# One decoder layer on one core: order of the products of the first two quads, and of norm, transposes and splits in the output projection

## The chip, the cores and the metric

The kernel runs on one core of a Trainium2 chip, in one program. The metric is the time of one execution on the device in microseconds (us); the time of a kernel is the median of its runs. A core has five engines with a queue of instructions each: TensorE (PE in the profile, with its weight loads as PEld), VectorE (DVE), ScalarE (ACT), GpSimd (POOL) and SyncE (SP, which here only issues transfers). An engine works its queue off in order, and an instruction waits until the instructions of other engines that it depends on have ended.

## The reference

One layer of a decoder with 512 tokens and a model width of 1024, in float32. Only the last third matters here:

```python
mixed = (sigmoid(gate_a) * (o_nsa @ w_branch_a) + sigmoid(gate_b) * (z @ w_branch_b))
x = x + mixed @ w_out                       # output projection, 512x1024 @ 1024x1024
h = rms_norm(x, norm2_g)
return x + square(relu(h @ w_up)) @ w_down  # D_FF = 4096
```

## The kernel before

Each float32 operand is kept as a high part and a low part, and each product of two operands is three matmuls (`mm3`, lines 230 to 232): high by high, high by low, low by high. A weight is loaded by SyncE into `w_raw`; ScalarE copies it into `w_hi` (line 87) and VectorE subtracts to get `w_lo` (line 89). This pair is called a split below. The weights of the last two stages are split in one piece of 128x1024.

The order of all work is the order in which the Python code emits it (a manual schedule): each engine gets its instructions in the order of the text, and the places are fixed by hand. `later(k, f)` emits `f` k slots on; in the quads a slot is one step of three matmuls, and a product of a quad is 8 slots.

**Output projection** (`tok_gemm`, `o_second`, `h_chunk`). The second half of its columns is computed token chunk by token chunk (c = 0 to 3, 128 tokens each, 24 matmuls of 512 columns). When chunk c is done, `after` is `o_second`: VectorE adds the residual (`x`, line 857), ScalarE squares and sums (line 905), small operations make the scale `st` (lines 907, 193 to 195) and VectorE writes the normed chunk `hn` (line 909). `mid(c - 1)` is `h_chunk` of the chunk before: TensorE transposes `hn` into `ptr` (line 919, 8 transposes, two PSUM tiles), ScalarE copies them to `ht` and `hA` (lines 922, 927) and VectorE subtracts for the low part of `hA` (line 928). For c = 1 and 2 `mid(c - 1)` is emitted at the end of product c and ahead of `after(c)`; for c = 3 it is emitted after three quarters of the product. Four splits of weights of the next stage are emitted at (c, kp) = (2, 1), (2, 3), (3, 0) and (3, 1).

**Up stage** (`up_group`, class `Quad`). The up and down matmuls use a seven-product scheme (Strassen-Winograd): a quad makes four blocks of h @ w_up from seven products p1 to p7 of 24 matmuls of 256 columns each. Three accumulators in PSUM carry them: `y` takes p1, p6, p7 and p4 one on top of the other, `z` takes p5 and p3, `x` takes p2. Between two products on the same accumulator its value is read out: `keep` copies it (p1, p5 and u2; line 1002, ScalarE), and `block` subtracts (line 1026, VectorE) and then queues square, high part and low part of the result (lines 1011 to 1020). So a product that goes on in `y` or `z` waits until ScalarE's copy or VectorE's block has read it. Group 0 (g = 0) has two quads a and b that are interleaved, because their input `h` is not ready at the start: the sums S1 to S4 of parts of `h` (`h_sum`, line 934, in `ht`) and their high and low parts (`h_parts`, lines 938 and 939, in `hS`) are made while p1 and p2 of both quads run. Then the products follow as a.p5, a.p6, a.p3, a.p7, b.p5, a.p4, b.p6, b.p3, b.p7, b.p4. The blocks of a quad lie in one tile `G` with a single buffer, so b's first write to `G` waits for a's last read of it; the block of p2 lies in `a11` (two buffers). After p4 four sums over blocks (S1, S2, S4, S3; line 1070, VectorE) make the inputs of the down stage, `uh` and `ul`.

**Down stage** (`st_down`): the same scheme with matmuls of 512 columns, accumulators `dacc`. Groups 1 to 3 follow in the same way, one quad after the other.

Of the kernel before, what the change touches and what calls it, by code (L numbers as in the profile page):

```python
# [104 lines left out]
def layer(tc, flat, sizes, x, cst, wck, wcv, g1, g2, out):  # L105
# [36 lines left out]
    for g in range(4):  # L142
        for what in ("u", "d"):
            b11, b12, b21, b22 = (W.dram(2048) for _ in range(4))
            t1, t2, t3, t4 = t = [
                dr.tile([P, 2048], F32, name=f"t{what}{k + 1}_{g}") for k in range(4)
            ]
            sums.append([[m[:, v : v + 1024] for m in (b11, b12, b22, b21, *t)]
                         for v in (0, 1024)])

            def half(c, *ms):
                return [m[:, c * 1024 : (c + 1) * 1024] for m in ms]

            if what == "d":
                for m in (b11, b21, t1, t2, b22, t3, t4):
                    W.plan += half(0, m) + half(1, m)
            elif g:
                for c in range(2):
                    W.plan += half(c, b11, t1, t2, b22, t3, b21, t4)
            else:  # L160
                W.plan += half(0, b11, b21) + half(1, b11, b21) + half(0, t1, t2, b22, t3)
                W.plan += half(1, t1) + half(0, t4) + half(1, t2, b22, t3, t4)


    xs = [sp.tile([P, DM], F32, name=f"x{c}") for c in range(NT)]
# [62 lines left out]
    def mm3(ps, a, b, start, stop, **kw):  # L228

        nc.tensor.matmul(ps, a[0], b[0], start=start, stop=False, **kw)  # L230
        nc.tensor.matmul(ps, a[0], b[1], start=False, stop=False, **kw)  # L231
        nc.tensor.matmul(ps, a[1], b[0], start=False, stop=stop, **kw)  # L232
# [624 lines left out]
        nc.vector.tensor_tensor(v, ps, v, ALU.add)  # L857
        return v

    def tok_gemm(ci, act, after, tok_outer, last=False, mid=None):  # L860

        if not tok_outer:
            acc = [ps_acc.tile([P, 512], F32, name="acc", tag="acc") for _ in range(NT)]
            for kp in range(4):
                hi, lo = W.get(ci + kp)
                W.split_to(ci + kp + 2)
                for k in range(2):
                    ko = 2 * kp + k
                    w = slice(k * 512, (k + 1) * 512)
                    tick(2.9)  # L870
                    for c in range(NT):
                        mm3(acc[c], part(act, ko, c), (hi[:, w], lo[:, w]),
                            ko == 0, ko == NKO - 1)
                        if ko == NKO - 1:
                            after(c, acc[c])
        else:
            for c in range(NT):
                parts = 2 if last and c == NT - 1 else 1
                for b in range(parts):
                    n = 512 // parts  # L880
                    ps = ps_acc.tile([P, 512], F32, name="acc", tag="acc")
                    for kp in range(4):
                        hi, lo = W.get(ci + kp)
                        for k in range(2):
                            ko = 2 * kp + k
                            w = slice(k * 512 + b * n, k * 512 + (b + 1) * n)
                            mm3(ps[:, :n], part(act, ko, c), (hi[:, w], lo[:, w]),
                                ko == 0, ko == NKO - 1)
                        tick(1.45 / parts)
                        if (c, kp) in ((2, 1), (2, 3), (3, 0), (3, 1)):  # L890
                            W.split_to(W.ns)
                        if kp == (2 if c == NT - 1 else 3) and b == parts - 1 and c:
                            mid(c - 1)
                    if parts == 1:
                        after(c, ps)
                    else:
                        after(c, ps[:, :n], b * n, n)

    def o_first(c, ps):
        v = res_add(c, 0, ps)  # L900
# [74 lines left out]
    class Quad:  # L975
# [48 lines left out]
        def block(self, v, d, a, b, op, k=0):  # L1024

            nc.vector.tensor_tensor(d, a, b, op)  # L1026
            later(2, lambda: self.square(d))
            later(4 + k, lambda: self.high(v, d))
            later(6 + k, lambda: self.low(v, d))

# [22 lines left out]

        def p7(self):
            self.mm(self.y, S3, False)
            self.block(A22, self.g(A22), self.t["p5"], self.y, ALU.subtract)

        def p4(self):
            self.mm(self.y, A22, False)
            a21 = self.g(S3)  # L1060
            nc.scalar.activation(a21, self.y, AF.Relu)
            if self.q < 2:
                nc.scalar.activation(a21, a21, AF.Square)
            else:
                nc.vector.scalar_tensor_tensor(
                    a21, self.y, 0.0, a21, op0=ALU.max, op1=ALU.mult
                )

            def sum_(d, a, b, op):
                nc.vector.tensor_tensor(self.g(d), a, b, op)  # L1070

            def parts(k, a, b=None):
                v = slice(a, (b or a) + 1)
                src = self.G[:, :, v.start - 1 : v.stop - 1, :]
                later(k, lambda: self.high(v, src))
                later(k + 2, lambda: self.low(v, src))

            later(1, lambda: sum_(S1, a21, self.g(A22), ALU.subtract))
            later(3, lambda: sum_(S2, self.g(S1), self.a11, ALU.subtract))
            parts(4, S1)  # L1080
            later(5, lambda: sum_(S4, self.g(S2), self.g(A12), ALU.add))
            later(7, lambda: sum_(S3, self.a11, a21, ALU.subtract))
            parts(9, S2, S4)
            parts(11, S3)
# [4 lines left out]
    def up_group(g):  # L1089
        each[0] = 0.36  # L1090
        a, b = Quad(2 * g), None
        if g:
            for q in range(2):
                a = a or Quad(2 * g + q)
                for f in (a.p1, a.p5, a.p6, a.p3, a.p7, a.p2, a.p4):
                    f()
                a = None
            return

        t2, t3 = slice(0, P), slice(P, 2 * P)  # L1100
        later(3, lambda: h_parts(S1, t2))
        later(5, lambda: h_sum(S3, 0, 2, ALU.subtract, t2))
        a.p1()
        a.p2(24)
        b = Quad(1)
        h_chunk(NT - 1)
        h_sum(S1, 2, 3, ALU.subtract, t3)
        h_parts(S1, t3)
        later(3, lambda: h_sum(S3, 0, 2, ALU.subtract, t3))
        later(5, lambda: h_sum(S2, 3, 0, ALU.subtract))  # L1110
        later(7, lambda: h_parts(S2))
        later(10, lambda: h_sum(S4, 0, 1, ALU.add))
        later(12, lambda: h_parts(S4))
        later(15, lambda: h_parts(S3))
        later(16, open_act)
        b.p1()
        b.p2(24)
        for f in (a.p5, a.p6, a.p3, a.p7, b.p5, a.p4, b.p6, b.p3, b.p7, b.p4):
            f()

    def st_down(ci, last):
# [181 lines left out]
```

## Time and profile before

| | before |
|---|---|
| time, median of 3 runs | 821.95 us (820.93 to 822.28) |
| the profiled execution, its own time | 820.94 us |
| span of the profiled execution, first to last instruction | 819.2 us |
| busy time of TensorE / VectorE / ScalarE | 790.5 / 585.3 / 396.2 us |

The span lies 1.7 us inside the execution's own time, and this execution is 1.0 us under the median. Times in rows are microseconds from the start of the span. A matmul's duration in a row holds its pipeline; the distance of two starts is what a matmul costs: a row of 256 columns lasts 0.28 us, and the next one starts 0.12 us after it.

### The profile page before, as it was taken

To read this page: it belongs to the slowest core of one execution; us is meant where nothing else is said; L and a number is where in the kernel's file an instruction comes from. 1 tells how busy PE (TensorE), PEld (TensorE's weight loads), DVE (VectorE), ACT (ScalarE), POOL (GpSimd) and SP (SyncE) were. 2 spreads that over 40 slices of the span, in tenths; PEclk is the share of its full clock that TensorE was granted. 3 is DMA by queue.
4 is the path that set the end of the run, shared out by engine and by line. 5 is a ranking of instruction groups with operands and counts; after the bars stand their busy time and mean duration, and the time that the engine had idled before them with its cause. 6 is when DMAs were issued, how large, how long until landed. Compare 5 with 4: busy or idle time off the path is not lost.

```text
span 819.2 us, 11917 instructions
## 1 busy us (share of the span) xinstructions
PE 790.5 (97%) x4421; PEld 681.2 (83%) x4421; DVE 585.3 (71%) x1005; ACT 396.2 (48%) x714; POOL 88.2 (11%) x138
## 2 busy tenths in 40 slices
PE   5999989999999999999999987979999999999998
PEld 4898868888888788888888777968998899889987
DVE  6577887666767466665666478778599769967984
ACT  5544645545455353223223456863465446535651
POOL 0011573224323200000000000000000000000000
PEclk9999999999999999999999999989999999999999
DMA  9346568568757749999999822537988995565562
GB/s 343 122 133 202 139 130 207 173 159 171 193 154 133 175 120 323 317 323 324 349 324 319 324 83 98 180 129 217 290 254 260 255 268 192 186 199 189 181 208 78
DMA packets 49450, 172.56 MB, mean 211 GB/s; under 512 B 5616, under 2 KB 6000, under 8 KB 49392
## 3 DMA queue, kind: packets, MB, share of 16 engines
q1 hardware_dynamic: 42768, 148.14, 52.8%
q0 software_dynamic: 4608, 16.78, 13.3%
q10 hardware_dynamic: 2016, 6.88, 2.4%
q8 instruction: 35, 0.57, 0.3%
q14 instruction: 23, 0.19, 0.1%
HBM read 152.90 MB, written 52.43 MB: 251 GB/s over the span
## 4 chain that ended last, share of the span: by engine, by line
PE 86%; DVE 7%; ACT 4%; issue 1%; DMA 1%; POOL 0%; SPq 0%; ACTq 0%; DVEq 0%; POOLq 0%
PE acc L230 14%; PE acc L232 14%; PE acc L231 14%; PE dacc L230 6%; PE dacc L232 6%; PE dacc L231 6%; PE uacc L230 4%; PE uacc L231 4%; PE uacc L232 4%; PE ptu L687 2%; PE sc L640 2%; PE uz L230 2%; PE uz L231 2%; PE uz L232 2%; PE pv L711 1%
## 5 line engine op out<-in xcount | busy, mean ns | idle before, releaser
L89 DVE TENSOR_TENSOR w_lo<-w_raw,w_hi 128x512 fp32r<-128x512 f32 (+3 forms) x268 | 233.9, 887 | 76.9 <-ACT w_hi L87 76.1
L87 ACT ACTIVATE w_hi<-w_raw 128x512 fp32r<-128x512 f32 (+3 forms) x268 | 201.3, 778 | 99.7 <-PE dacc L232 71.1
L230 PE MATMUL acc<-xh,w_hi 128*128 128x512 f32 x336 | 137.5, 409 | 0.0
L232 PE MATMUL acc<-xh,w_lo 128*128 128x512 f32 x336 | 131.7, 392 | 0.0
L231 PE MATMUL acc<-xl,w_hi 128*128 128x512 f32 x336 | 131.1, 390 | 0.0
L231 PE MATMUL dacc<-w_lo,uh 128*128 128x512 f32 (+1 forms) x228 | 87.9, 386 | 0.0
L230 PE MATMUL dacc<-w_hi,uh 128*128 128x512 f32 (+1 forms) x228 | 87.9, 386 | 0.0
L232 PE MATMUL dacc<-w_hi,ul 128*128 128x512 f32 (+1 forms) x228 | 87.8, 385 | 0.0
L232 PEld LDWEIGHTS acc<-xh,w_lo 128*128 128x128 f32 x336 | 63.0, 188 | 14.3
L230 PEld LDWEIGHTS acc<-xh,w_hi 128*128 128x128 f32 x336 | 63.2, 188 | 11.8 <-issue 3.2
L231 PEld LDWEIGHTS acc<-xl,w_hi 128*128 128x128 f32 x336 | 63.3, 188 | 8.0
L230 PE MATMUL uacc<-hA,w_hi 128*128 128x256 f32 x192 | 55.4, 289 | 4.7 <-DVE G L1026 4.7
L652 ACT ACTIVATE p<-p,nst 128x512 f32<-128x512 f32 (+2 forms) x48 | 29.6, 616 | 55.7 <-DVE nst L648 54.5
L231 PE MATMUL uacc<-hA,w_hi 128*128 128x256 f32 x192 | 55.2, 288 | 0.0
L232 PE MATMUL uacc<-hA,w_lo 128*128 128x256 f32 x192 | 55.2, 288 | 0.0
L232 PEld LDWEIGHTS dacc<-w_hi,ul 128*128 128x128 f32 x228 | 42.8, 188 | 8.7
L231 PEld LDWEIGHTS dacc<-w_lo,uh 128*128 128x128 f32 x228 | 42.8, 188 | 8.5
L230 PEld LDWEIGHTS dacc<-w_hi,uh 128*128 128x128 f32 x228 | 42.8, 188 | 8.4
L1132 DVE TENSOR_TENSOR x<-x,dacc 128x512 f32<-128x512 f32 (+1 forms) x57 | 36.8, 673 | 11.5 <-PE dacc L232 11.5
L693 DVE TENSOR_TENSOR pt<-ptu,pt 128x384 fp32r<-128x384 f32 (+1 forms) x48 | 28.8, 600 | 19.6 <-ACT pt L692 19.5
L668 POOL TENSOR_SCALAR p<-p,nst 128x512 f32<-128x512 f32 (+2 forms) x48 | 32.8, 690 | 88.6 <-DVE nst L666 43.5
L230 PEld LDWEIGHTS uacc<-hA,w_hi 128*128 128x128 f32 x192 | 37.8, 197 | 5.0 <-DVE G L1026 4.9
(231 smaller groups left out, 1659.4 us busy)
## 6 DMA issues: line engine op xcount, KB each, us to landing
w_raw<-w_flat SPq DMA_DIRECT2D x110, 512.0 KB, 4.7
w_raw<-tu SPq DMA_DIRECT2D x32, 512.0 KB, 4.8
w_raw<-td SPq DMA_DIRECT2D x32, 512.0 KB, 4.7
tu<-w_flat SPq DMA_DIRECT2D x16, 512.0 KB, 6.3
z<-w_flat SPq DMA_DIRECT2D x16, 512.0 KB, 6.8
tu<-w_flat POOLq DMA_DIRECT2D x8, 512.0 KB, 7.5
tu<-tu POOLq DMA_DIRECT2D x8, 512.0 KB, 9.6
td<-w_flat SPq DMA_DIRECT2D x8, 512.0 KB, 5.5
```

What stands on the lines that cost most here:

```text
L87: nc.scalar.activation(hi[:, v], t[:, v], AF.Copy)
L89: nc.vector.tensor_tensor(lo[:, v], t[:, v], hi[:, v].bitcast(F32), ALU.subtract)
L230: nc.tensor.matmul(ps, a[0], b[0], start=start, stop=False, **kw)
L231: nc.tensor.matmul(ps, a[0], b[1], start=False, stop=False, **kw)
L232: nc.tensor.matmul(ps, a[1], b[0], start=False, stop=stop, **kw)
L640: nc.tensor.matmul(ps[:, : b - a], QS[h][:, t], ks[h // 4][:, a:b], start=k == 0, stop=k == 1)
L652: later(1, lambda: nc.scalar.activation(p, p, AF.Exp, scale=-1.0, bias=mn, accum_out=sm))
L668: nc.gpsimd.tensor_scalar(p_of(u, k), p_of(u, k), nst[:, u % 4, 1, k : k + 1], 1.0, op0=ALU.mult, op1=ALU.mult,)
L687: nc.tensor.transpose(pt[:, n : n + P], p_of(u, c)[:, k * P : (k + 1) * P], ident)
L693: later(1, lambda: nc.vector.tensor_tensor(ptl[:, at], pt[:, :n], pth[:, at].bitcast(F32), ALU.subtract))
L711: nc.tensor.matmul(pv[:HD, q0:], v[:, :HD], ptl[:, at : at + w], start=False, stop=False)
L1132: nc.vector.tensor_tensor(v, v, ps[:, o : o + n], op)
```

## The change

1. In the output projection `mid(c - 1)` now comes behind `after(c)` for c = 1 and 2, and the splits are three instead of four, at (2, 0), (2, 1) and (3, 0). The unused handling of a half product is dropped.
2. The products of group 0 go a.p5, a.p6, a.p3, a.p7, b.p5, **b.p6, a.p4, b.p7, b.p3**, b.p4; the order in which the weights are loaded (`W.plan`) is changed to match.
3. `block` queues the square 2 + k // 2 slots on instead of 2. Only p2 of quads a and b has k = 24, so the squares of their first rows (`a11`) come 14 slots on.
4. The block of p7 goes into a tile `a22` of its own instead of a place in `G`, in all quads.

```diff
-                W.plan += half(1, t1) + half(0, t4) + half(1, t2, b22, t3, t4)
+                W.plan += half(1, t1, t2) + half(0, t4) + half(1, t3, b22, t4)
...
-                        if (c, kp) in ((2, 1), (2, 3), (3, 0), (3, 1)):
-                            W.split_to(W.ns)
-                        if kp == (2 if c == NT - 1 else 3) and b == parts - 1 and c:
-                            mid(c - 1)
-                    if parts == 1:
-                        after(c, ps)
-                    else:
-                        after(c, ps[:, :n], b * n, n)
+                    if (c, kp) in ((2, 0), (2, 1), (3, 0)):
+                        W.split_to(W.ns)
+                    if (c, kp) == (NT - 1, 2):
+                        mid(c - 1)
+                after(c, ps)
+                if 0 < c < NT - 1:
+                    mid(c - 1)
...
-            later(2, lambda: self.square(d))
+            later(2 + k // 2, lambda: self.square(d))
...
-            self.block(A22, self.g(A22), self.t["p5"], self.y, ALU.subtract)
+            self.a22 = gp2.tile([P, 2, 256], F32, name="a22", tag="a22")
+            self.block(A22, self.a22, self.t["p5"], self.y, ALU.subtract)
...
-            later(1, lambda: sum_(S1, a21, self.g(A22), ALU.subtract))
+            later(1, lambda: sum_(S1, a21, self.a22, ALU.subtract))
...
-        for f in (a.p5, a.p6, a.p3, a.p7, b.p5, a.p4, b.p6, b.p3, b.p7, b.p4):
+        for f in (a.p5, a.p6, a.p3, a.p7, b.p5, b.p6, a.p4, b.p7, b.p3, b.p4):
```

TensorE's own order in the output projection stays as it is, since `after` has no work for it. What moves there is VectorE's and ScalarE's order. VectorE's queue around the third chunk (`x_2`, `hn_4102`; `hn_4103` is the second chunk), before:

```order
L909 SCALAR_TENSOR_TENSOR hn_4103<-x_1_4094,st_4107,g2b 128x1024
L89 TENSOR_TENSOR w_lo<-w_raw,w_hi 128x1024 x2
L928 TENSOR_TENSOR hA_4092<-ptr,hA_4091 128x2x2x128 x2
L857 TENSOR_TENSOR x_2_4095<-acc,x_2_4095 128x512
L907 TENSOR_TENSOR st_4107<-st_4107 128x1
L193 TENSOR_SCALAR st_4107<-st_4107 128x1
L195 RECIPROCAL st_4107<-st_4107 128x1
L909 SCALAR_TENSOR_TENSOR hn_4102<-x_2_4095,st_4107,g2b 128x1024
L89 TENSOR_TENSOR w_lo<-w_raw,w_hi 128x1024 x2
```

and the same place of the changed kernel (its lines 857 and 89 are the same, 904 is the old 909, 923 the old 928):

```order
L904 SCALAR_TENSOR_TENSOR hn_4103<-x_1_4094,st_4107,g2b 128x1024
L923 TENSOR_TENSOR hA_4092<-ptr,hA_4091 128x2x2x128 x2
L89 TENSOR_TENSOR w_lo<-w_raw,w_hi 128x1024 x2
L857 TENSOR_TENSOR x_2_4095<-acc,x_2_4095 128x512
L902 TENSOR_TENSOR st_4107<-st_4107 128x1
L193 TENSOR_SCALAR st_4107<-st_4107 128x1
L195 RECIPROCAL st_4107<-st_4107 128x1
L904 SCALAR_TENSOR_TENSOR hn_4102<-x_2_4095,st_4107,g2b 128x1024
L923 TENSOR_TENSOR hA_4092<-ptr,hA_4091 128x2x2x128 x2
```

The `hA` pair ahead of `x_2` is that of the second chunk's transposes before, and of the first chunk's now; the second chunk's pair has moved behind `hn` of the third.

ScalarE's queue in the up stage, from the squares of a's first rows (`a_4557`) to the copy of a.p5's accumulator (`p_4694<-uz`), before; `a_4659` are b's first rows, and the three `hS` of 1024 elements are the high parts of S2, S4 and S3:

```order
L1011 ACTIVATE a_4557<-a_4557 128x512
L1012 ACTIVATE a_4557<-a_4557 128x512
L938 ACTIVATE hS_4491<-ht 128x1024
L1002 ACTIVATE p_4616<-uacc 128x512
L87 ACTIVATE w_hi<-w_raw 128x1024
L938 ACTIVATE hS_4491<-ht 128x1024 x2
L87 ACTIVATE w_hi<-w_raw 128x1024
L1011 ACTIVATE a_4659<-a_4659 128x512
L1012 ACTIVATE a_4659<-a_4659 128x512
L1002 ACTIVATE p_4694<-uz 128x512
```

and of the changed kernel, where `p_4692<-uz` is that copy and lines 1006 and 1007 are the squares:

```order
L933 ACTIVATE hS_4485<-ht 128x1024
L997 ACTIVATE p_4614<-uacc 128x512
L87 ACTIVATE w_hi<-w_raw 128x1024
L933 ACTIVATE hS_4485<-ht 128x1024
L1006 ACTIVATE a_4557<-a_4557 128x512
L1007 ACTIVATE a_4557<-a_4557 128x512
L933 ACTIVATE hS_4485<-ht 128x1024
L87 ACTIVATE w_hi<-w_raw 128x1024
L997 ACTIVATE p_4692<-uz 128x512
L87 ACTIVATE w_hi<-w_raw 128x1024
L1012 ACTIVATE uh<-a_4557 128x2x256
L1006 ACTIVATE a_4659<-a_4659 128x512
```

The squares of b's first rows have moved from ahead of the copy to behind it, and those of a's first rows from ahead of the high part of S2 to behind that of S4.

VectorE's queue between a's sums and b.p4, before; `G<-a_4557,G` is a's last sum, `G<-uz,u_4904` the block of b.p3 and `G<-p_4834,uacc` the block of b.p7, which b.p4 waits for:

```order
L1070 TENSOR_TENSOR G<-G 128x2x256
L1020 TENSOR_TENSOR ul<-G,uh 128x2x256
L1070 TENSOR_TENSOR G<-a_4557,G 128x2x256
L89 TENSOR_TENSOR w_lo<-w_raw,w_hi 128x1024
L1020 TENSOR_TENSOR ul<-G,uh 128x2x512
L1020 TENSOR_TENSOR ul<-G,uh 128x2x256
L1026 TENSOR_TENSOR G<-uz,u_4904 128x2x256
L89 TENSOR_TENSOR w_lo<-w_raw,w_hi 128x1024
L1020 TENSOR_TENSOR ul<-G,uh 128x2x256
L1026 TENSOR_TENSOR G<-p_4834,uacc 128x2x256
```

and of the changed kernel, where `a_4937<-p_4835,uacc` is the block of b.p7 and lines 1066 and 1015 are the old 1070 and 1020:

```order
L1066 TENSOR_TENSOR G<-G 128x2x256
L1015 TENSOR_TENSOR ul<-G,uh 128x2x256
L1066 TENSOR_TENSOR G<-a_4557,G 128x2x256
L1021 TENSOR_TENSOR a_4937<-p_4835,uacc 128x512
L89 TENSOR_TENSOR w_lo<-w_raw,w_hi 128x1024
L1015 TENSOR_TENSOR ul<-G,uh 128x2x512
L1015 TENSOR_TENSOR ul<-G,uh 128x2x256
L1015 TENSOR_TENSOR ul<-a_4937,uh 128x2x256
L1021 TENSOR_TENSOR G<-uz,u_4867 128x2x256
```

The block of b.p7 now stands directly behind a's last sum and ahead of the block of b.p3.

## Rows read from the trace of the kernel before

**Rows 1.** The page: the chain that ended last, shares by engine.
```profile
PE 86%; DVE 7%; ACT 4%; issue 1%; DMA 1%; POOL 0%; SPq 0%; ACTq 0%; DVEq 0%; POOLq 0%
```

**Rows 2.** Waits of PE, 430 to 580 us: total, times, longest.
```profile
PE uacc L230 <- DVE G L1026: 4.7, 1, 4.7
PE uz L230 <- ACT p L1002: 4.1, 1, 4.1
PE ptr L919 <- DVE hn L909: 2.3, 2, 1.9
PE uacc L231 <- DVE hS L939: 0.8, 1, 0.8
```

**Rows 3.** Windows: length, busy PE, PEld, DVE, ACT, POOL, granted clock, DMA.
```profile
486.90:488.80 1.90, 1.89 (x13) 1.72 (x14) 1.90 (x2) 1.47 (x4) 0.00 (x0) 1.00 0.03 9
512.50:515.90 3.40, 3.38 (x16) 3.38 (x17) 2.33 (x3) 2.87 (x4) 0.00 (x0) 0.53 0.52 167
538.70:543.40 4.70, 4.61 (x21) 4.62 (x22) 1.86 (x3) 1.89 (x3) 0.00 (x0) 0.50 0.46 157
488.80:543.80 55.00, 45.42 (x348) 44.73 (x347) 41.65 (x53) 36.95 (x56) 0.00 (x0) 0.91 0.44 144
```

**Rows 4.** Timeline, output projection: start, length, engine, line, operation, idle before.
```profile
472.70 1.03 PE L919 MATMUL ptr<-ident,hn 128*128 128x128 f32 x8
474.45 0.69 DVE L928 TENSOR_TENSOR hA<-ptr,hA 128x512 fp32r<-128x512 f32 x1 [2.67 <-ACT hA L927]
476.04 0.68 DVE L857 TENSOR_TENSOR x<-acc,x 128x512 f32<-128x512 f32 x1
479.53 2.35 DVE L89 TENSOR_TENSOR w_lo<-w_raw,w_hi 128x1024 fp32r<-128x1024 f32 x2
479.76 1.07 PE L919 MATMUL ptr<-ident,hn 128*128 128x128 f32 x8 [0.42 <-DVE hn L909]
481.80 1.42 DVE L928 TENSOR_TENSOR hA<-ptr,hA 128x512 fp32r<-128x512 f32 x2
483.13 0.68 DVE L857 TENSOR_TENSOR x<-acc,x 128x512 f32<-128x512 f32 x1
485.48 1.28 DVE L909 SCALAR_TENSOR_TENSOR hn<-x,st,g2b 128x1024 f32<-128x1024 f32 x1
486.91 1.06 PE L919 MATMUL ptr<-ident,hn 128*128 128x128 f32 x8 [1.89 <-DVE hn L909]
```

**Rows 5.** Timeline, from S4's sum over the copy of a.p5 to a.p3.
```profile
505.35 1.22 DVE L934 TENSOR_TENSOR ht<-ht 128x1024 f32<-128x1024 f32 x1
506.60 2.01 ACT L938 ACTIVATE hS<-ht 128x1024 fp32r<-128x1024 f32 x2 [1.00 <-DVE ht L934]
508.17 0.28 PE L232 MATMUL uacc<-hS,w_lo 128*128 128x256 f32 x1
510.69 0.63 ACT L1011 ACTIVATE a<-a 128x512 f32<-128x512 f32 x1 [1.14 <-DVE a L1026]
511.89 0.58 ACT L1002 ACTIVATE p<-uz 128x512 f32<-128x512 f32 x1
512.52 0.47 PE L230 MATMUL uz<-hS,w_hi 128*128 128x256 f32 x1 [4.08 <-ACT p L1002]
516.99 0.28 PE L230 MATMUL uacc<-hS,w_hi 128*128 128x256 f32 x1
```

**Rows 6.** Timeline, ends of a.p4 and b.p7, a's last sum, b.p4, down stage.
```profile
525.37 0.28 PE L232 MATMUL uacc<-hA,w_lo 128*128 128x256 f32 x1
531.01 0.69 DVE L1070 TENSOR_TENSOR G<-a,G 128x512 f32<-128x512 f32 x1
533.82 0.28 PE L232 MATMUL uacc<-hS,w_lo 128*128 128x256 f32 x1
538.79 0.58 PE L230 MATMUL uacc<-hA,w_hi 128*128 128x256 f32 x1 [4.69 <-DVE G L1026]
543.78 0.40 PE L230 MATMUL dacc<-w_hi,uh 128*128 128x512 f32 x1
```

More of the change, by code (lines that the diff above doesn't have):

```diff
@@ L858, in res_add, with tok_gemm @@
         return v
-    def tok_gemm(ci, act, after, tok_outer, last=False, mid=None):
+    def tok_gemm(ci, act, after, tok_outer, mid=None):
         if not tok_outer:
@@ L877, in tok_gemm @@
             for c in range(NT):
[L878 to L889, printed above, removed]
-                        if (c, kp) in ((2, 1), (2, 3), (3, 0), (3, 1)):
-                            W.split_to(W.ns)
-                        if kp == (2 if c == NT - 1 else 3) and b == parts - 1 and c:
-                            mid(c - 1)
-                    if parts == 1:
-                        after(c, ps)
-                    else:
-                        after(c, ps[:, :n], b * n, n)
+                ps = ps_acc.tile([P, 512], F32, name="acc", tag="acc")
+                for kp in range(4):
+                    hi, lo = W.get(ci + kp)
+                    for k in range(2):
+                        ko = 2 * kp + k
+                        w = slice(k * 512, (k + 1) * 512)
+                        mm3(ps, part(act, ko, c), (hi[:, w], lo[:, w]), ko == 0, ko == NKO - 1)
+                    tick(1.45)
+                    if (c, kp) in ((2, 0), (2, 1), (3, 0)):
[5 more added lines that the diff above has]
+                    mid(c - 1)
     def o_first(c, ps):
```

## The prediction

> **What bounds the kernel now.** I read the page first, then the waits of TensorE, then the granted clock around each wait, then the timeline of the engines that end it. The chain that ended last lies to 86% on TensorE [rows 1], so only what shortens TensorE's stretch counts. Between 430 and 580 us, the stretch that the change touches, TensorE waits four times over: 2.3 us in two waits for `hn` in the output projection, 0.8 us for the low part of S2, 4.1 us for ScalarE's copy of a.p5 and 4.7 us for a block on VectorE, that of b.p7 [rows 2]; 11.9 us in all. None of these waits names a transfer. The reader should see in the windows what else they cost: after the 4.1 us the granted clock is 0.53 for 3.4 us and after the 4.7 us it is 0.50 for 4.7 us, which is the lower level of 1.2 GHz; after the wait of 1.9 us it stays at 1.00, 2.4 GHz [rows 3].
>
> **How long a product takes.** From a.p4's last matmul (start 525.37) to that of b.p7 (533.82) lie three products: 8.45 / 3 = 2.82 us at full clock [rows 6]. a.p3, begun at the low clock, takes 516.99 - 512.52 = 4.47 us, so 1.65 more [rows 5]; b.p4, low nearly throughout, takes 543.78 - 538.79 = 4.99 us, so 2.17 more [rows 6].
>
> **Part 1, the output projection: 2.1 us of waits go.** Before, VectorE stands idle 2.67 us for the `hA` of the first chunk, while the second product, whose transposes of chunk 0 begin at 472.70, is done and its residual add is queued behind; it runs at 476.04 [rows 4]. Now the add goes first, at about 472.75, 3.3 us earlier. The second chunk's `hn` ended at about 479.65 (TensorE took it at 479.76 after 0.42 us of waiting [rows 4]), so it will end at 476.35 and that wait is gone. Then VectorE has an `hA` pair (1.42) and two splits (2.35) [rows 4] up to 480.1, and the third add starts there. From add to end of `hn` is 485.48 + 1.28 - 483.13 = 3.63 us [rows 4]: 483.7. TensorE comes to the transposes at 486.91 - 1.89 - 0.42 = 484.6, so the 1.89 us are covered by 0.9. What is late next is the second chunk's `hA` pair, now behind that `hn`: it ends at 485.1, and the second PSUM tile of transposes is wanted about then. I leave 0.2 us for it and take 2.3 - 0.2 = 2.1 us, between 1.9 and 2.3.
>
> **Part 2, the split that leaves the projection: up to 1.1 us back.** Three splits instead of four means that the fourth lands on VectorE between the last `hn` and the sums of `h`, at 2.27 / 2 = 1.13 us (start to start of the split pair and the next instruction [rows 4]). The sums feed S2 and with it a.p6, which already waits 0.8 us for them [rows 2]. So the chain of sums comes earlier by 2.1 - 1.13 = 1.0 us if VectorE had no slack there, and by 2.1 us if it had enough. VectorE also waits for ScalarE in this chain, which takes up part of it, so I take the middle, 1.5 us. a.p6 then goes on 1.5 us earlier than before, after 0.6 us more of waiting, and its last matmul ends its slot at 508.17 + 0.12 - 1.5 = 506.8.
>
> **Part 3, the squares 12 slots on: a.p3 starts 2.7 us earlier.** Before, ScalarE's copy of a.p5 stands behind the squares of b's first rows, which wait 1.14 us for VectorE [rows 5]. They go behind it; in exchange the squares of a's first rows come in between. S4's sum ends at 505.35 + 1.22 - 1.5 = 505.07; then ScalarE has the high part of S4 from 505.12, 0.96 (the pair takes 506.60 to 508.51), the two squares of a, 1.20 (510.69 to 511.89), the high part of S3, 0.96, a split, 0.96 (same size), and the copy, 0.58 [rows 5]: it ends at 509.77. TensorE starts a.p3 at 509.8 and not at 512.52: 2.7 us earlier, after a wait of 3.0 us from slot to slot where it was 4.2. So this wait shrinks by no more than 1.2 us; the rest of the 2.7 is the 1.5 from before.
>
> **Part 4, the order of the products: 3.6 us of wait, and 2.2 us of low clock.** Before, b.p7 and b.p4 stand side by side on `y`, and b.p7's block comes last on VectorE, behind the block of b.p3, which needs a's `G` free. TensorE waits 4.85 us from slot to slot (533.94 to 538.79 [rows 6]). Now b.p7 follows a.p4, b.p3 lies between it and b.p4, and its block has a tile of its own, right behind a's last sum. That sum starts 531.01 - 525.49 = 5.5 us after a.p4's slot ends, and the block is done at most 0.69 + 0.69 later: 6.9 us after a.p4. TensorE has two products in the meantime, 5.64 us. So it waits up to 1.3 us, since two VectorE instructions overlap a little I take 1.2, and not 4.85. Since the clock stayed up after 1.9 us [rows 3], it should stay up here, and b.p4 takes 2.82 us: 2.2 saved. The chain runs from a.p4's own end, so nothing that comes earlier changes it. The other reads are covered: a.p4 has b.p5 and b.p6 between it and a.p7's block, b.p7 has a.p4 between it and b.p6's copy. b.p3's block now comes late for its square and split, but the down stage reads these rows only after b.p4 and three chunks of its own (a's and b's A11, a's A12), which covers it.
>
> **Other edits.** Two loads swap places on SyncE's queue with the weights, and one load starts a split later; no wait of TensorE is for a load [rows 2], so nothing. The tile of p7's block changes no duration. In groups 1 to 3 it has four products before its next use: nothing.
>
> **Sum.** 2.7 (parts 1 to 3, as a.p3's start) + 3.6 + 2.2 = 8.5 us. Against the profiled execution's own 820.94 us that is 812.4; this execution lies 1.0 us under the median of 821.95, against which I forecast: **813.4 us**, with a.p3 at the low clock as before. Its own bounds are 7.5 and 9.5 us, from parts 1 and 2.
>
> **The clock after the 3.0 us wait.** The rows have a wait of 1.9 us, clock kept, and one of 4.1, clock lost [rows 2, 3]; 3.0 lies between and decides nothing. The Trainium skill ("TensorE: Matmul & The Clock Gate", section "Part 1: The HAM clock gate") says that the throttled clock is the default and activity releases it. That agrees with the 0.53 and 0.50 behind the long waits, while the 1.00 behind 1.9 us shows that not every wait lets the throttle in; by the rule alone every wait could, which is rival 2.
>
> **Rivals.** (1) The clock stays up at a.p3: 1.65 us more. But a.p3 is then done at 509.8 + 2.82 = 512.6, and a.p7 meets the copy `u2`, ahead of which the squares of b now stand: from 509.7 ScalarE has a split 0.96, a high part 0.53, the squares 1.20 and the copy 0.58 (half a high part and the rest as in part 3), which ends at 513.0. So 0.4 us go back: 812.2 us. (2) The clock falls at b.p4 too, after 1.2 us of waiting: it costs that product 2.17 us as now, 815.6 us. The row with 1.9 us and 1.00 speaks against it [rows 3]. (3) VectorE becomes the bound: it is busy 41.65 of 55.0 us in the two quads [rows 3], and with the split more and 6.4 us less it would be 42.9 of 48.6, 88%. If for that b.p7's block comes no earlier than now, the wait of 4.85 us and its low clock stay, only 2.7 us are left: 819.3. Against it speaks that the block no longer stands behind a release of `G`. (4) Slower: the clock does not come back after a.p3, because products at half speed and the copies they wait for follow each other. Then the seven products up to b.p4 cost 2.17 us each, 15.2, less the 1.2 us wait that they hide: 8.5 + 1.2 - 15.2 = 5.5 us slower, 827.5. It decides from five such products on (9.7 / 2.17 = 4.5). Against it: after both long waits the clock was back within 3.4 and 4.7 us of matmuls [rows 3]. (5) The reordering does nothing, because the engines' queues have the same relative order: the queues of the changed kernel show the moves, so hardly.
>
> **Chances and range.** Forecast (813.4) 0.47, rival 1 (812.2) 0.29, rival 2 (815.6) 0.05, rival 3 (819.3) 0.10, rival 4 (827.5) 0.04, no change 0.02, better than all of these 0.03. The range reaches from rival 1 with the upper bound of parts 1 and 2 (811.2) to rival 2 with the lower bound (816.6); since runs of the kernel before lie up to 1.0 us under their median, I go 0.4 lower: 810.8 to 816.6, with rivals 3 to 5, 0.16, and part of the best case outside. Within 0.2%, 1.6 us, a measurement of this kernel can't tell a change from none; by that faster is 0.93 (rival 3 counts to it with 2.7 us), same 0.03, slower 0.04.
>
> **What would show it.** Of the changed kernel: no wait for `hn` over 0.2 us; a.p6's wait for `hS` 1 to 1.6 us; a.p3's wait for the copy near 2.9 us; b.p4's wait for a VectorE block near 1.1 us with granted clock 1.00 behind it. The prediction is wrong if b.p4 waits for 3 us or more, if a wait appears in the down stage, or if the clock is at 0.5 for more than about 5 us of the two quads.

## The result and the profile after

The changed kernel takes **811.96 us** (median; 810.78 to 813.01), the kernel before beside it 821.61 us: ratio 0.9882, 95% interval 0.9865 to 0.9899, so about 9.7 us or 1.2% faster. Measured again beside the kernel before, the difference of the medians was 9.8 us (e1) and 8.5 us (e12). The forecast was 813.4 us with a range of 810.8 to 816.6. The profiled execution of after took 812.05 us with a span of 810.2 us.

Most readings below are distances inside one execution, since the stretch ahead of the change varies by about 2 us between executions. The clock starts at R: VectorE's residual add of the first token chunk in the second half of the output projection's columns. Nothing that the change touches comes before it. R in the timelines of before and of after, and the last matmul of after (the last of before starts at 815.64):

```profile
467.30 0.69 DVE L857 TENSOR_TENSOR x<-acc,x 128x512 f32<-128x512 f32 x1 [1.13 <-PE acc L232]
```

```profile
466.66 0.69 DVE L857 TENSOR_TENSOR x<-acc,x 128x512 f32<-128x512 f32 x1 [1.12 <-PE acc L232]
...
806.72 0.28 PE L232 MATMUL dacc<-w_hi,ul 128*128 128x256 f32 x1
```

After was already 0.64 us earlier at R, which is no work of the change. From R to the last matmul it is 340.06 us instead of 348.34: 8.28 us are the change's.

The page of after, busy times and the chain that ended last:

```profile
PE 788.4 (97%) x4421; PEld 678.8 (84%) x4421; DVE 584.6 (72%) x1005; ACT 395.3 (49%) x714; POOL 88.4 (11%) x138
...
PE 86%; DVE 6%; ACT 4%; issue 2%; DMA 1%; POOL 0%; SPq 0%; ACTq 0%; DVEq 0%; POOLq 0%
```

The waits of TensorE from 420 to 580 us (total, times, longest), which answer [rows 2]:

```profile
PE uz L230 <- ACT p L997: 2.8, 1, 2.8
PE uacc L230 <- DVE a L1021: 1.2, 1, 1.2
PE uacc L231 <- DVE hS L934: 0.9, 1, 0.9
PE uacc L230 <- ACT hS L933: 0.4, 1, 0.4
```

The waits for `hn` are gone, the copy of a.p5 makes TensorE wait 2.8 us instead of 4.1, the block ahead of b.p4 1.2 instead of 4.7, and S2 takes 0.5 us more: 5.3 us instead of 11.9. The windows, in the columns of [rows 3]: a.p3, from there to b.p4, b.p4, all behind it, and all from R to the end of b.p4:

```profile
509.10:513.66 4.56, 4.56 (x26) 4.56 (x27) 3.75 (x5) 4.18 (x7) 0.00 (x0) 0.63 0.43 120
513.66:531.90 18.24, 17.09 (x144) 16.90 (x144) 13.75 (x18) 13.87 (x20) 0.00 (x0) 1.00 0.60 201
531.90:534.80 2.90, 2.88 (x24) 2.90 (x25) 2.90 (x4) 2.87 (x5) 0.00 (x0) 1.00 0.25 79
534.80:806.80 272.00, 272.00 (x1694) 246.18 (x1693) 220.85 (x264) 142.04 (x164) 6.47 (x8) 1.00 0.69 215
466.66:534.80 68.14, 62.88 (x440) 58.21 (x439) 52.64 (x72) 47.53 (x77) 0.00 (x0) 0.97 0.39 129
```

b.p4 now runs at the upper level (1.00, it was 0.50 in [rows 3]); a.p3 still falls to the lower one. Behind b.p4 TensorE is busy throughout, so nothing was given back in the down stage.

The output projection, which answers [rows 4] (VectorE, and TensorE's transposes):

```profile
472.26 0.69 DVE L857 TENSOR_TENSOR x<-acc,x 128x512 f32<-128x512 f32 x1 [1.12 <-PE acc L232]
...
478.54 1.03 PE L914 MATMUL ptr<-ident,hn 128*128 128x128 f32 x8
...
479.53 0.68 DVE L857 TENSOR_TENSOR x<-acc,x 128x512 f32<-128x512 f32 x1
...
481.88 1.28 DVE L904 SCALAR_TENSOR_TENSOR hn<-x,st,g2b 128x1024 f32<-128x1024 f32 x1
483.08 1.28 DVE L923 TENSOR_TENSOR hA<-ptr,hA 128x512 fp32r<-128x512 f32 x2
...
483.82 1.25 PE L914 MATMUL ptr<-ident,hn 128*128 128x128 f32 x8
```

The second and third adds start 5.60 and 12.87 us after R; the forecast had them at 472.75 and 480.1 of before's time, 5.45 and 12.8 after R. Neither group of transposes shows a wait; the second lasts 1.25 instead of 1.06 us, the 0.2 us that the forecast left for the pair of `hA`.

ScalarE's chain to a.p3, which answers [rows 5], with TensorE's first matmul of a.p3:

```profile
504.41 1.06 ACT L933 ACTIVATE hS<-ht 128x1024 fp32r<-128x1024 f32 x1 [1.00 <-DVE ht L929]
505.38 0.62 ACT L1006 ACTIVATE a<-a 128x512 f32<-128x512 f32 x1
506.02 0.63 ACT L1007 ACTIVATE a<-a 128x512 f32<-128x512 f32 x1
506.56 1.04 ACT L933 ACTIVATE hS<-ht 128x1024 fp32r<-128x1024 f32 x1
507.51 1.04 ACT L87 ACTIVATE w_hi<-w_raw 128x1024 fp32r<-128x1024 f32 x1
508.45 0.57 ACT L997 ACTIVATE p<-uz 128x512 f32<-128x512 f32 x1
...
509.08 0.38 PE L230 MATMUL uz<-hS,w_hi 128*128 128x256 f32 x1 [2.82 <-ACT p L997]
```

From the high part of S4 to the copy this is the queue of the forecast, link by link, without a gap: the copy is late by what stands ahead of it, which e3 and e7 below test. VectorE's chain to b.p4, which answers [rows 6]:

```profile
526.46 0.69 DVE L1066 TENSOR_TENSOR G<-G,a 128x512 f32<-128x512 f32 x1 [1.37 <-ACT G L1059]
527.41 1.23 DVE L89 TENSOR_TENSOR w_lo<-w_raw,w_hi 128x1024 fp32r<-128x1024 f32 x1 [0.26 <-ACT w_hi L87]
528.55 0.69 DVE L1066 TENSOR_TENSOR G<-G,a 128x512 f32<-128x512 f32 x1
...
530.49 0.69 DVE L1066 TENSOR_TENSOR G<-a,G 128x512 f32<-128x512 f32 x1
531.09 0.68 DVE L1021 TENSOR_TENSOR a<-p,uacc 128x512 f32<-128x512 f32 x1
...
531.92 0.35 PE L230 MATMUL uacc<-hA,w_hi 128*128 128x256 f32 x1 [1.17 <-DVE a L1021]
```

b.p7's block (531.09, into its own tile) stands right behind a's last sum (530.49), and b.p4 waits for it 1.17 us.

### The profile page after: what moved, and what is told of

Read it like the earlier page. It is cut to its first block, busy times and chain, and to the rows that moved or that the text cites. A ratio compares the mean times of both kernels' runs of the same rounds, so it can differ in the third digit from the quotient of the medians.

```text
span 810.2 us, 11914 instructions
## 1 busy us (share of the span) xinstructions
PE 788.4 (97%) x4421; PEld 678.8 (84%) x4421; DVE 584.6 (72%) x1005; ACT 395.3 (49%) x714; POOL 88.4 (11%) x138
## 4 chain that ended last, share of the span: by engine, by line
PE 86%; DVE 6%; ACT 4%; issue 2%; DMA 1%; POOL 0%; SPq 0%; ACTq 0%; DVEq 0%; POOLq 0%
PE acc L230 14%; PE acc L232 14%; PE acc L231 14%; PE dacc L230 6%; PE dacc L231 6%; PE dacc L232 6%; PE uacc L230 4%; PE uacc L232 4%; PE uacc L231 4%; PE ptu L687 2%; PE sc L640 2%; PE uz L230 2%; PE uz L232 2%; PE uz L231 2%; PE pv L711 1%
## 5 line engine op out<-in xcount | busy, mean ns | idle before, releaser
L230 PE MATMUL uacc<-hA,w_hi 128*128 128x256 f32 x192 | 54.4, 283 | 1.2 <-DVE a L1021 1.2
L231 PE MATMUL uacc<-hA,w_hi 128*128 128x256 f32 x192 | 54.3, 283 | 0.0
L295 POOL DMA_DIRECT2D td<-w_flat x8 | 6.5, 844 | 310.9 <-DMA td<-w_flat 310.9
```

## The experiments

All times in us. "to a.p3", "to b.p4" and "to the end" are the starts of the first matmul of a.p3, of b.p4 and of the last matmul, less the start of R, in each kernel's profiled execution (after: 509.08 - 466.66 = 42.42). "Clock at a.p3" says whether the granted clock fell there: over the 4.5 us from a.p3's start it is 0.62 to 0.65 where it fell and 1.00 where it stayed. The ratio is that of the times to the kernel before on the same chip, with its interval; e1 to e4 ran on one chip, e5 to e8 on a second, e9 to e12 on a third.

| kernel | to a.p3 | to b.p4 | to the end | clock at a.p3 | time | ratio |
|---|---|---|---|---|---|---|
| before | 45.22 | 71.49 | 348.34 | fell | 821.95 | |
| changed | 42.42 | 65.26 | 340.06 | fell | 811.96 | 0.9882 (0.9865 to 0.9899) |
| changed (e1) | 42.43 | 65.28 | 340.08 | fell | 811.46 | 0.9881 (0.9866 to 0.9897) |
| changed (e12) | 42.43 | 65.17 | 339.97 | fell | 812.59 | 0.9900 (0.9884 to 0.9916) |
| old order of products (e2) | 42.44 | 68.55 | 344.87 | stayed | 817.79 | 0.9961 (0.9949 to 0.9973) |
| old squares (e3) | 43.69 | 66.53 | 341.33 | fell | 814.30 | 0.9917 (0.9903 to 0.9931) |
| old projection, 4 splits (e4) | 43.97 | 65.60 | 340.41 | stayed | 814.29 | 0.9916 (0.9902 to 0.9930) |
| old projection, 3 splits (e5) | 44.88 | 67.62 | 342.43 | fell | 814.95 | 0.9925 (0.9912 to 0.9938) |
| new projection, 4 splits (e6) | 42.29 | 65.13 | 340.43 | fell | 812.39 | 0.9894 (0.9881 to 0.9908) |
| squares 25 slots on (e7) | 41.25 | 62.92 | 337.72 | stayed | 809.78 | 0.9865 (0.9850 to 0.9880) |
| the same (e11) | 41.25 | 62.90 | 337.71 | stayed | 810.26 | 0.9867 (0.9851 to 0.9884) |
| that and sums later (e8) | 41.26 | 61.70 | 338.22 | stayed | 810.70 | 0.9871 (0.9856 to 0.9886) |
| order alone, on before (e9) | 45.23 | 68.04 | 342.85 | fell | 815.23 | 0.9932 (0.9915 to 0.9948) |
| changed, sums later (e10) | 42.43 | 62.72 | 338.90 | stayed | 811.91 | 0.9889 (0.9873 to 0.9906) |

The distances repeat to 0.1 us (changed, e1 and e12), the medians to about 1 us; so where both speak, the distances say where and the medians say that it is there at all. The distances are those of one execution each, and whether the clock fell at a.p3 changes between executions of the same kernel: in e1 the mean granted clock of the whole execution is 0.998 and 0.997 in two (812.32 and 811.10 us) and 1.000 in the other two (811.82 and 810.18 us).

**The theory** is that of the prediction: three chains in in-order queues (`hn`, the copy of a.p5, the block ahead of b.p4) set the time, each part of the change shortens one, and they add up. **The rival** is that VectorE's amount of work is the limit, so that what one place gains another gives back.

### The changed kernel again

> The changed kernel once more, beside the next three on the same chip, as what they are measured against. 812.0 us, ratio 0.988 to the kernel before; TensorE's waits in the first two quads 0.4 and 0.9 us for the parts of S2, 2.8 us for the copy of a.p5 and 1.2 us for the block ahead of b.p4.

> The changed kernel a third time, beside the three others: 811.6 us, a.p3 42.4 us and b.p4 64.1 to 65.3 us after the first chunk's residual add, by whether the clock falls behind the wait of 2.8 us.

811.46 and 812.59 us; waits and distances as in the first trace, so it serves as the measure for the others. In all three the clock fell at a.p3.

### The old order of the products

```diff
-                W.plan += half(1, t1, t2) + half(0, t4) + half(1, t3, b22, t4)
+                W.plan += half(1, t1) + half(0, t4) + half(1, t2, b22, t3, t4)
...
-        for f in (a.p5, a.p6, a.p3, a.p7, b.p5, b.p6, a.p4, b.p7, b.p3, b.p4):
+        for f in (a.p5, a.p6, a.p3, a.p7, b.p5, a.p4, b.p6, b.p3, b.p7, b.p4):
```

> The changed kernel with the old order of the products and of the two loads; p7's block keeps its own tile, squares and output projection stay as changed. Theory (part 4 of the prediction): b.p7's block stands behind b.p3's block again, which needs a's last read of G; b.p4 waits 4.7 us instead of 1.2 and the clock falls to the lower level behind it: 3.5 + 2.2 = 5.7 us slower than the changed kernel, 817.7 us. Rival (VectorE's amount of work, not its order, set that wait): everything ahead of it comes 2.8 us earlier already, so the wait stays near 1.2 to 2 us, 812 to 813 us. Second rival (the wait comes back but the clock does not fall, because the tile of its own lets the block go a little earlier): 815.5 us.

817.79 us, and the wait is back in full although everything ahead of it comes 2.8 us earlier than in before. Its wait of PE for the blocks (total, times, longest):

```profile
PE uacc L230 <- DVE a L1021: 5.5, 2, 4.7
```

Its window of b.p4 (granted clock 0.67):

```profile
536.20:541.30 5.10, 5.02 (x27) 4.93 (x28) 1.85 (x3) 2.25 (x4) 0.00 (x0) 0.67 0.45 149
```

The first matmuls of a.p4 and b.p4 in its timeline:

```profile
520.01 0.36 PE L230 MATMUL uacc<-hA,w_hi 128*128 128x256 f32 x1 [0.78 <-DVE a L1021]
...
536.28 0.39 PE L230 MATMUL uacc<-hA,w_hi 128*128 128x256 f32 x1 [4.71 <-DVE a L1021]
```

The theory's number (817.7) is met and the rivals' (812 to 813, 815.5) are not: the order sets this wait. By the distances the order is worth 4.81 us here, with the clock up at a.p3, which is worth up to 1.2 us (below). The row at 520.01 shows that the old order could not use those 1.2: with only b.p5 between a.p7 and a.p4, TensorE came earlier to a.p7's block and waited 0.78 us for it. e2 keeps the tile of its own for p7's block, and its wait is 4.71 us against 4.69 in before: that tile alone doesn't shorten it.

### The new order alone, on the kernel before

```diff
-                W.plan += half(1, t1) + half(0, t4) + half(1, t2, b22, t3, t4)
+                W.plan += half(1, t1, t2) + half(0, t4) + half(1, t3, b22, t4)
...
-            self.block(A22, self.g(A22), self.t["p5"], self.y, ALU.subtract)
+            self.a22 = gp2.tile([P, 2, 256], F32, name="a22", tag="a22")
+            self.block(A22, self.a22, self.t["p5"], self.y, ALU.subtract)
...
-        for f in (a.p5, a.p6, a.p3, a.p7, b.p5, a.p4, b.p6, b.p3, b.p7, b.p4):
+        for f in (a.p5, a.p6, a.p3, a.p7, b.p5, b.p6, a.p4, b.p7, b.p3, b.p4):
```

> The kernel before with the new order of the products, of its two loads and p7's block in a tile of its own, and nothing else. Theory (part 4, worth the same with or without the other parts): b.p4 waits 1.2 us instead of 4.7 and runs at 1.00; the waits for hn (2.3 us), S2 (0.8) and the copy of a.p5 (4.1, low clock behind it) stay. From the first chunk's residual add to b.p4 68.0 us instead of 71.5, and 5.7 us faster than the kernel before: 815.2 to 815.6 us. Rival (VectorE is full without the earlier projection): b.p4 waits 2.5 us or more, 70 us to b.p4, 817 us or more.

815.23 us. The first matmul of b.p4 in the timeline:

```profile
535.65 0.35 PE L230 MATMUL uacc<-hA,w_hi 128*128 128x256 f32 x1 [1.17 <-DVE a L1026]
```

The window of b.p4:

```profile
535.60:538.50 2.90, 2.85 (x24) 2.88 (x25) 2.90 (x4) 2.87 (x5) 0.00 (x0) 1.00 0.29 71
```

The same 1.17 us of wait and the clock at 1.00, without the other parts: from a.p3 to b.p4 it is 22.81 us (before 26.27, changed 22.84), to the end 5.49 us less. The whole change's 8.28 less 5.49 leaves 2.79 for the rest, and a.p3 starts 2.80 earlier: the parts add up. The rival would have had b.p4 wait 2.5 us or more here, and falls. The new order without the tile of its own wasn't run, so whether the order needs it stays open.

### The old squares

```diff
-            later(2 + k // 2, lambda: self.square(d))
+            later(2, lambda: self.square(d))
```

> The changed kernel with all squares queued 2 slots on, as before. Theory (part 3): ScalarE's copy of a.p5 stands behind the squares of b's first rows again; a.p3's wait goes from 2.8 to 4.0 us, the clock falls behind it in both cases: 1.2 us slower than the changed kernel, 813.2 us. Rival (squares that leave the copy's front only make place for the squares of a, so that nothing is gained): 812.0 us, with a.p3's wait at 2.8 us. Second rival (a longer low stretch as well): 814 us or more.

814.30 us. The first matmul of a.p3 in the timeline:

```profile
510.69 0.38 PE L230 MATMUL uz<-hS,w_hi 128*128 128x256 f32 x1 [4.07 <-ACT p L997]
```

The wait is 4.07 instead of 2.82 us and a.p3 1.27 us later, and 1.27 us later it stays to the end: theory 1.2. The median lies 2.8 us above that of the changed kernel beside it, 1.5 more than the trace. As a number it is the second rival's (814 or more, a longer low stretch). In the profiled execution (813.63 us) that isn't so: the matmuls are at the lower level from 511.9 to 515.1, in after from 510.2 to 513.6. But the mean granted clock is 0.998 there and 0.996 in three of the other four executions, and in e1 1.000 in two of four. So the clock can make part of the 1.5, on both sides; how much isn't shown.

### The output projection: its order and its splits

Old order and four splits (e4, all of the function `tok_gemm` as before):

> The changed kernel with the old order of norm, transposes and four splits in the output projection. Theory (parts 1 and 2): the two waits for hn of 0.4 and 1.9 us come back, a.p6's wait for S2 falls from 1.3 to 0.8 us or less, and a.p3 starts 1.5 us later: 1.5 us slower than the changed kernel, 813.5 us. Rival (what the projection gains is lost again at S2 and at the copy of a.p5, since one more split lies ahead of them): 812.0 us, with the waits for hn 2.3 us back and 2.3 us less of waiting at a.p6 and a.p3. Second rival (none of it is lost): 814.3 us.

Old order and three splits (e5):

```diff
-                after(c, ps)
                 if 0 < c < NT - 1:
                     mid(c - 1)
+                after(c, ps)
```

> The changed kernel with the transposes of chunk c - 1 again ahead of the residual add and norm of chunk c, but with the three splits where the change has them. Theory (part 1: the order of norm and transposes is what gains): the waits for hn of 0.4 and 1.9 us come back and a.p3 starts 2.1 to 2.4 us later, 45 us after the residual add of the first chunk instead of 42.4; 2.3 us slower than the changed kernel. Rival (the fourth split that left is what gains): waits for hn stay small or are made good at a.p6, a.p3 within 0.5 us of the changed kernel.

New order and four splits (e6):

```diff
-                    if (c, kp) in ((2, 0), (2, 1), (3, 0)):
+                    if (c, kp) in ((2, 0), (2, 1), (3, 0), (3, 1)):
```

> The changed kernel with a fourth split of weights in the output projection, at (3, 1) as before. Theory (part 2: the fourth split, behind the last hn, costs the sums of h 0.6 us, at most 1.1): a.p6's wait for S2 falls from 1.3 us by that much and a.p3 starts 0.6 to 1.1 us earlier, 41.3 to 41.8 us after the first chunk's residual add. Rival (the split only changes sides: ahead of the last hn it delays that as much): 42.2 to 42.4 us, no difference in time.

As a median e4 (814.29 us) lies on the number of its second rival (814.3, none of the 2.3 us lost). Its distance to a.p3 doesn't: 1.55 us more than the changed kernel, where the theory had 1.5 and the rival 2.3. In e5 a.p3 is 2.46 us later and the last matmul 2.37, as its theory had it (2.3). The theory of e6 (a.p3 0.6 to 1.1 us earlier) was missed.

The waits for `hn` are back in e4 and e5 (2.3 us in total, 1.9 the longest, in both). The line of PE's waits in e5:

```profile
PE ptr L914 <- DVE hn L904: 2.3, 2, 1.9
```

With the changed kernel this makes a square of four, from R to a.p3: old order 43.97 with four splits and 44.88 with three; new order 42.29 and 42.42. Both edits together are worth 1.55 us, as the theory had it. But by this square all of it is the order: 1.68 us with four splits, 2.46 with three. Taking the fourth split out of the projection costs 0.91 us in the old order and 0.13 in the new one. The square isn't quite clean: in e4 the two splits of the third chunk stand at (2, 1) and (2, 3), in the other three kernels at (2, 0) and (2, 1), so the 1.68 and the 0.91 hold that move too. So the rival was right for e6 (42.2 to 42.4): behind the new order the split fits on either side, and this edit of the change gains nothing.

By the distances e4 loses only 0.35 us to the end, because its a.p3 ran at the upper clock. Its first matmul in the timeline:

```profile
511.77 0.38 PE L230 MATMUL uz<-hS,w_hi 128*128 128x256 f32 x1 [2.79 <-ACT p L1002]
```

The window from there on:

```profile
511.70:515.00 3.30, 3.20 (x25) 2.99 (x25) 3.30 (x4) 3.27 (x7) 0.00 (x0) 1.00 0.16 52
```

From a.p3 to b.p4 e4 takes 21.63 us, the changed kernel with its fall 22.84: that is the price of the fall, **1.21 us**, behind the same wait of 2.8 us.

### Past the change: squares later still, sums later

Squares 25 slots on (e7, and again beside the changed kernel as e11):

```diff
-            later(2 + k // 2, lambda: self.square(d))
+            later(2 + 23 * k // 24, lambda: self.square(d))
```

> The changed kernel with the squares of the first rows 25 slots on instead of 14, so that those of a leave the front of the copy of a.p5 too. Theory (ScalarE's queue ahead of that copy is the wait): 1.2 us less, a.p3's wait 1.6 us instead of 2.8, and at that length the clock stays at 1.00 as behind the 1.9 us before: together 1.2 to 2.4 us faster than the changed kernel, 809.3 to 810.5 us. Rival (what is late next takes it): the copy waits for the high part of S3 or the copy u2 waits behind the squares, and less than 0.5 us is left.

> The kernel with the squares 25 slots on once more, beside the changed kernel on the same chip. 1.2 us faster than the changed kernel where its clock stays up at a.p3, 2.4 us where it falls: 809.2 to 810.4 us; a.p3 41.25 us after the first chunk's residual add, clock 1.00 throughout the two quads. Against it: a load that lands late at the first down stage takes back up to 1.1 us.

809.78 and 810.26 us, the best of this study; e11's times (809.06 to 811.04) and e12's of the changed kernel (812.27 to 813.85), on the same chip, don't overlap. The first matmuls of a.p3 and a.p7 in e7's timeline:

```profile
507.22 0.39 PE L230 MATMUL uz<-hS,w_hi 128*128 128x256 f32 x1 [1.64 <-ACT p L997]
...
510.52 0.39 PE L230 MATMUL uacc<-hS,w_hi 128*128 128x256 f32 x1 [0.18 <-ACT u L997]
```

Its window from R to the end of b.p4:

```profile
465.97:531.80 65.83, 61.55 (x440) 56.68 (x439) 52.60 (x72) 47.42 (x77) 0.00 (x0) 1.00 0.41 133
```

The two squares of a leave the front of the copy, 506.56 - 505.38 = 1.18 us in the rows of after, and a.p3 starts 1.17 us earlier. The clock stays at 1.00: another 1.17 to b.p4, 2.34 to the end. Only 0.18 us of wait for the copy `u2` are new. One of the other three executions of e7 (811.42 us, its slowest) has a mean granted clock of 0.998, like those of the changed kernel with a fall; e11's four have 1.000.

a's sums S4 and S3 4 slots later, with the squares 25 slots on (e8) and without (e10):

```diff
-            later(5, lambda: sum_(S4, self.g(S2), self.g(A12), ALU.add))
-            later(7, lambda: sum_(S3, self.a11, a21, ALU.subtract))
-            parts(9, S2, S4)
-            parts(11, S3)
+            w = 4 if self.q == 0 else 0
+            later(5 + w, lambda: sum_(S4, self.g(S2), self.g(A12), ALU.add))
+            later(7 + w, lambda: sum_(S3, self.a11, a21, ALU.subtract))
+            parts(9 + w, S2, S4)
+            parts(11 + w // 2, S3)
```

> As the kernel with the squares 25 slots on, and in addition the sums S4 and S3 of a's blocks (with their high and low parts) 4 slots later, so that they come behind the block of b.p7 on VectorE. Theory: b.p4's wait of 1.2 us goes to 0, 1.2 us faster than with the squares alone, 808 to 809.3 us. Rival (the sums are wanted by the down stage, or VectorE is full by then): a wait of 0.5 to 1.2 us at the first down products, and no gain beyond that of the squares.

> The changed kernel with a's sums S4 and S3 4 slots later, squares 14 slots on as in the change. Theory (b.p4's last wait is a's two sums on VectorE): b.p4's wait is gone, 64.1 us from the first chunk's residual add to b.p4 instead of 65.3, and since TensorE comes to the down stage no earlier than with the squares 25 slots on (62.9), the loads keep up there: 1.2 us faster than the changed kernel, 810.4 us. Rival (VectorE or the loads limit the first down stage whenever the sums are late): a wait of 0.5 to 1.1 us at a down product again, and less than 0.5 us is left.

810.70 and 811.91 us, and by the distances no gain: to the end e8 takes 338.22 us and e7 337.72; e10 takes 338.90, and the changed kernel's 340.06 less the price of its fall (1.21; e10's clock stayed up) is 338.85. b.p4's wait is gone in both. b.p4 starts 1.2 us earlier than in e7 (e8), and 2.5 us earlier than in the changed kernel (e10), about half of it by the clock. But from b.p4 to the end it takes 276.52 us in e8 and 276.18 in e10, where the changed kernel and e7 need 274.80. The timeline of e8 in group 0's down stage, a split on ScalarE and a matmul:

```profile
563.11 1.06 ACT L87 ACTIVATE w_hi<-w_raw 128x1024 fp32r<-128x1024 f32 x1 [5.05 <-DMA w_raw<-td]
...
566.17 0.47 PE L230 MATMUL dacc<-w_hi,uh 128*128 128x512 f32 x1 [1.06 <-DVE x L1129]
```

The same split in the timeline of e10:

```profile
563.64 1.06 ACT L87 ACTIVATE w_hi<-w_raw 128x1024 fp32r<-128x1024 f32 x1 [4.64 <-DMA w_raw<-td]
```

The wait of PE in e10's down stage:

```profile
PE dacc L230 <- DVE x L1129: 0.6, 1, 0.6
```

The releaser named is VectorE, whose residual add stands behind a low part that waited for that split; the split waited for a load of down weights, 5.05 and 4.64 us. The rival named for both is what came: the first down stage takes the gain. SyncE's issue of four such loads in e7 and in e8:

```profile
544.27 6.66 SPq L63 DMA_DIRECT2D w_raw<-td  x4
```

```profile
545.84 6.65 SPq L63 DMA_DIRECT2D w_raw<-td  x4
```

That is 15.4 us behind b.p4's start in e7, and so in the changed kernel, but 16.9 us behind it in e8, and so in e10: b.p4 came earlier and these loads did not. That the later sums make the load late isn't shown by this: e6, without them and with its loads 15.4 us behind b.p4, has the same load 4.2 us late, 0.2 us of wait at the same place, and 275.30 us from b.p4 to the end, while e7 and e11, where b.p4 starts only 0.2 us later than in e10, have none of it.

## Why the prediction was right, step by step

- **Part 1**, 2.1 us of `hn` waits gone and 0.2 left for the pair of `hA`: right, by the waits of after and the adds 5.60 and 12.87 us after R.
- **Part 2**, the moved split: the sum (a.p3's chain 1.5 us earlier) was right at 1.55, but of the two terms that made it the price of the split was mis-sized. It was put between nothing and 1.13 us, with 0.6 taken; it measures 0.13 beside the new order, and 0.91 where the old order stays (with the move of two splits in it). So this edit of the change earns nothing, and what a.p3's start gains here is, as far as the square shows, part 1's. a.p6's wait for S2 grew from 0.8 to 1.23 (0.35 + 0.88), inside the 1 to 1.6 foretold.
- **Part 3**, the squares: a.p3 2.80 us earlier (2.7 foretold), wait 2.82 (2.9 foretold), the squares alone 1.27 (1.2).
- **Part 4**, the order: b.p4's wait 1.17 us with the clock at 1.00 behind it (1.2 and 1.00 foretold). From a.p3 to b.p4 3.43 us saved (3.6), behind b.p4 2.05 (2.2).
- **Sum**: 2.80 + 3.43 + 2.05 = 8.28 us by the trace, 8.5 foretold. The experiments give the same for a.p3: 1.27 (e3) + 1.55 (e4) = 2.82. The profiled execution took 812.05 us where 812.4 was worked out, with 0.64 us of luck ahead of R in it. The remaining distance of the forecast, 813.4 against 811.96, is the step that added 1.0 us because before's profiled execution lay that far under its median; after's lies 0.1 above its own. The 9.7 us between the medians exceed the 8.28 by 1.4 us that no part of the change accounts for.
- **Rival 1**, the clock stays up at a.p3, 1.25 us better: it was given 0.29 against the forecast's fall, as if one of them held. Both hold: with the same wait of 2.8 us the clock fell in five profiled executions (changed, e1, e12, e5, e6) and stayed in three (e2, e4, e10). In time alone the result (811.96) lies nearer to this rival's 812.2 than to the forecast; that the clock fell is read from the traces. Its price was right in sum, 1.21, but not in its terms (1.65 for a.p3 less 0.4 at the copy `u2`): where the clock stayed the gap ahead of a.p7 is 0.2 (e4: starts at 514.61 and 514.92, 0.31 apart instead of 0.12), so the fall costs 1.4 and 0.2 go back.
- **Rivals 2 to 5**: rival 5, no effect, falls with the result; b.p4's window is at 1.00 in the changed kernel and in e9, so the clock doesn't fall behind 1.2 us; VectorE is no bound at b.p4 (e9); a.p3's low stretch ends by 513.66, and it is 1.00 from there to b.p4, so nothing builds up. A later stage takes a gain back only one step further on: in e8 and e10, at a load of the down stage and not by VectorE's amount of work.

## What to carry to other kernels

A wait that stays when its engine comes to it earlier is a matter of queue order: look at what stands in the queue between the producer's input and its output, and move what nobody waits for behind it. Two products that hand one accumulator to each other want other products between them, at least as long as the chain that reads the accumulator out. Where a shorter wait also keeps TensorE's clock up, it pays twice (e7: 1.17 us of wait and 1.17 of clock); where the next stage has no slack in its loads, it pays nothing (e8, e10).

## What the runs showed of the hardware

The granted clock behind a wait of TensorE, in the profiled executions: 1.00 after 1.2 us (changed, e9) and 1.6 us (e7, e11); low after 4.0 to 4.7 us each time (before twice, e3 and e9 at a.p3, e2 at b.p4; 0.62 or 0.63 over the 4.5 us from a.p3's start, 0.50 and 0.67 in the windows of b.p4 of before [rows 3] and of e2); and after 2.8 us low in five (0.62 to 0.65) and 1.00 in three, though e2, e10 and the changed kernel have the same work of TensorE up to there. Behind 1.6 us a fall isn't excluded, by the one execution of e7 with a mean clock of 0.998, which has no trace.

Where the clock fell, it did so at different moments. In e12, as in before (twice) and e9, the first matmuls behind the wait are already at the lower level:

```profile
509.61 0.58 PE L230 MATMUL uz<-hS,w_hi 128*128 128x256 f32 x1 [2.79 <-ACT p L997]
509.99 0.41 PE L231 MATMUL uz<-hS,w_hi 128*128 128x256 f32 x1
```

In after it fell later. Two rows of a.p3's matmuls before and behind the fall:

```profile
510.01 0.28 PE L231 MATMUL uz<-hS,w_hi 128*128 128x256 f32 x1
...
510.44 0.42 PE L231 MATMUL uz<-hS,w_hi 128*128 128x256 f32 x1
```

There TensorE had been at work again for over 1 us (from 509.08) at the upper level, and then went to the lower one; e1, e3 and e5 show the same, 1.0 to 1.3 us after the first matmul, and e6 within 0.4 us. The Trainium skill ("TensorE: Matmul & The Clock Gate", section "Part 1: The HAM clock gate") says that the throttled state is the default and that activity releases it. These rows agree that a wait can let the lower level in, and those of after show that activity right behind the wait does not yet keep it out.
